# One lo part in six of the experts' weights, made by GpSimd instead of VectorE

## The chip, the core and the metric

The kernel runs on one core of a Trainium2 chip. The metric is device time in microseconds (us), the median of several executions. In the profile PE is TensorE's matmul, PEld its weight load, DVE is VectorE, ACT is ScalarE, POOL is GpSimd, SP is SyncE, which issues the loads.

## What is computed

Two layers of a decoder trunk for 272 tokens of width 1024: three token mixers side by side, then a channel mixer, dense in the first layer and a mixture of eight experts in the second. The change touches the experts alone. Each token goes to its two best experts; each expert is a gated network of 1024 x 3584, 1024 x 3584 and 3584 x 1024 weights in float32.

```python
def swiglu(h, w_gate, w_up, w_down):
    return (jax.nn.silu(h @ w_gate) * (h @ w_up)) @ w_down

    out = jnp.zeros_like(h)
    for e in range(N_EXPERTS):
        out = out + combine[..., e:e + 1] * swiglu(h, w_gate[e], w_up[e], w_down[e])
```

## The kernel before

Matmuls run on a reduced float type (fp32r). To keep float32's precision each weight is split in two: hi, the weight rounded to that type, and lo, the rest (weight minus hi). ACT makes hi (line 856), DVE makes lo from the raw weight and hi (line 857), and TensorE multiplies with both.

The experts come one after another, sorted by how many tokens they have: first a wide one (up to 128 tokens), then a narrow and a wide one in turn, and a narrow one (up to 64 tokens) last: four wide and four narrow. Each expert has 7 chunks of 512 hidden columns. A chunk needs 6 loads of 1 MB: two halves each of gate, up and down, issued by SP into 7 raw buffers (`wr`). A load is cut into two parts of 128x1024, each of which is one hi, one lo and the matmuls on them. So a chunk has 12 parts, which the text calls g0a g0b g1a g1b u0a u0b u1a u1b for gate and up, and d0a d0b d2a d2b for down; the down parts of a chunk follow the gate and up parts of the next. The names in the program are h_g_0, l_g_0 and so on: h for hi, l for lo, and both parts of one load have the same name. There are 8 x 7 x 12 = 672 parts. hi and lo have 7 buffers each (`HB`), in two pools of 5 and 2, so hi of a part waits until TensorE is through with the part seven before it.

In a wide expert TensorE makes six matmuls of 512 columns per part, in a narrow one four. When the gate parts of a chunk are through, ACT copies their sum out of PSUM; then the same is done for up. In a narrow expert these copies are gs (line 1124) and us (line 1125); TensorE turns both (hps, line 1133), ACT takes the sigmoid-weighted half s (line 78), DVE multiplies (s, line 1136), and ACT and DVE split the result into hi and lo for the down products (ht, lines 1139 and 1140). In a wide expert the steps are h (lines 78 and 1097), hps (1104), hth (1108) and htl (1109). When an expert is through, its result is added to the tokens' sums (yh, yl, hst, lines 1075 to 1081).

Each engine works through its own list in order. The framework's scheduler writes these lists from its own estimate of durations, so an edit in one line can change the order on several engines. A second pass over the experts (line 1195) runs only if an expert has more tokens than its width; in the profiled execution it doesn't run.

`nparts[0]` counts the parts. GpSimd has nothing to do in the experts' stage; its work (lines 177, 503, 647 to 672, 696, 736) lies in the stages before.

Of the kernel before, what the change touches and what calls it, by code (L numbers as in the profile page):

```python
# [9 lines left out]
F32 = mybir.dt.float32  # L10
# [5 lines left out]
ALU = mybir.AluOpType  # L16
# [35 lines left out]
def trunk(ctx: ExitStack, tc: tile.TileContext, x, meta, n1g, n2g, w_in, qng, kng, dlam,  # L52
# [3 lines left out]
    V, A, G, PE = nc.vector, nc.scalar, nc.gpsimd, nc.tensor  # L56
# [8 lines left out]
    def raw_ins(i):  # L65
        return getattr(i, "ins", i)
# [50 lines left out]
    with ExitStack() as lctx:  # L117
# [233 lines left out]
        for l in range(2):  # L351
# [226 lines left out]
            for hp in range(0, NH, 2):  # L578

                lgs = {}  # L580
                for X in (TA, TB):
# [5 lines left out]
                    for m in range(2):  # L587
                        b = m * 2 + hp // 2
                        pss = [ptile("lgps") for _ in range(2)]
                        for i in range(2):  # L590
                            r = 64 * i
# [86 lines left out]
            for bi, b in enumerate((1, 2, 0)):  # L678
                for half in range(2):
                    w = Weights(w_branch[l, b, :, half * 512:half * 512 + 512].rearrange("(k p) c -> p k c", p=P),  # L680
                                4, 512, f"br{l}{b}{half}")
                    for qd in range(2):
                        hi, lo = w.part(slice(0, 4), slice(qd * 256, qd * 256 + 256))
# [95 lines left out]
            for fp in range(NFD // 2):  # L779
# [3 lines left out]
                for j in range(2):  # L783
                    pss = []
                    for w in (wg, wu):
                        hi, lo = w.part(slice(0, KD), slice(j * P, (j + 1) * P))
# [18 lines left out]
            for cg in range(4):  # L805
                ps2 = [pp.tile([P, 512], F32, tag="pp", name=f"dn{j}") for j in range(2)]
                for f0 in range(0, NFD, 8):
# [3 lines left out]
                    for j in range(2):  # L811
                        hi, lo = w.part(slice(0, nf), slice(j * P, (j + 1) * P))
# [24 lines left out]
    nparts = [0]  # L837
    EARLY = 5

    class MoveWeights:  # L840
# [7 lines left out]
        def parts(self):  # L848
            st = 1024 // self.cols
            for k0 in range(0, self.nk, st):  # L850
                late = nparts[0] % HB >= HB - LATE
                wq, nb_ = (wqs[0], LATE) if late else (wqs[1], HB - LATE)
                hi = wq.tile([P, st, self.cols], F32R, tag="hi", bufs=nb_, name="h_" + self.name)
                lo = wq.tile([P, st, self.cols], F32R, tag="lo", bufs=nb_, name="l_" + self.name)
                r = self.raw[:, k0:k0 + st, :]
                ih = raw_ins(A.activation(hi, r, AF.Copy))  # L856
                il = raw_ins(V.tensor_tensor(lo, r, hi.bitcast(F32), op=ALU.subtract))  # L857
                nparts[0] += 1
                if EARLY < nparts[0] < 16:

                    tc.add_manual_dep(il, routed[0].name, nosync, reason="router")
                if EARLY < nparts[0] < 16:
                    tc.add_manual_dep(ih, last_in[0].name, nosync, reason="router")
                for k in range(st):
                    yield k0 + k, hi[:, k, :], lo[:, k, :]
# [360 lines left out]
```

## Time and profile before

| what | value |
|---|---|
| median of 3 runs | 1828.93 us (1828.43 to 1829.12) |
| the profiled execution | 1831.06 us, its span 1829.3 us |
| PE busy / DVE busy | 1763.9 us (96%) / 1468.0 us (80%) |
| ACT busy / POOL busy | 1179.2 us (64%) / 110.4 us (6%) |
| lo parts of the experts, line 857 | 3 groups (g, u, d) x 224, 1220 ns mean each |
| hi parts of the experts, line 856 | 3 groups x 224, 1052 to 1053 ns mean each |
| loads of the experts | 1024 KB each, 7.0 to 7.9 us from issue to landing |

How to read it: the shares are means over the whole span. The experts take the second half of it, some 990 us, and there the engines are much nearer to one another than the means show. A matmul's busy time overlaps with that of the next one, so PE's share says little. What sets the pace is read stage by stage, from the time of one chunk and from what ends the waits in it.

### The profile page before, as it was taken

The page shows a single profiled execution, that of the slowest core. Times are in us where ns is not written, and L with a number is a line of the kernel's source. Part 1 is how long each engine was busy: PE and PEld are TensorE (multiplying, and loading weights), DVE is VectorE, ACT ScalarE, POOL GpSimd, SP SyncE. Part 2 cuts the span into 40 slices and gives each one's busy share as a digit, 9 for nine tenths or more (in the row PEclk, how much of TensorE's full clock was granted, in tenths as well). Part 3 has the DMA queues.
Part 4 walks back from the last instruction along what each step waited for, and adds up shares of the span by engine and source line. Part 5 has one row for each costly group of instructions (what it writes and reads, how often), then busy time and mean ns, then how long its engine had stood idle before and what let it go on. Part 6 is the DMA issues. An engine that isn't in the chain of part 4 may idle for free.

```text
span 1829.3 us, 27972 instructions
## 1 busy us (share of the span) xinstructions
PE 1763.9 (96%) x10613; PEld 1515.4 (83%) x10613; DVE 1468.0 (80%) x1934; ACT 1179.2 (64%) x1587; POOL 110.4 (6%) x137
## 2 busy tenths in 40 slices
PE   8999999999999999999999999999999999999997
PEld 7888999999999889998788767776677866787665
DVE  7667757877567577577889999989998899988997
ACT  4366444544443664446778887768877688877786
POOL 5201201100011003012000000000000000000000
PEclk9999999999999999998999999999999999999999
DMA  7333554555554236656989999999999899999996
GB/s 214 101 99 93 169 177 162 165 181 185 167 179 139 70 95 189 187 196 234 343 321 368 366 394 371 360 330 352 394 387 372 315 345 395 394 351 352 362 388 232
DMA packets 266123, 479.96 MB, mean 262 GB/s; under 512 B 7636, under 2 KB 115228, under 8 KB 265980
## 3 DMA queue, kind: packets, MB, share of 16 engines
q1 hardware_dynamic: 265472, 477.20, 73.8%
q8 instruction: 85, 1.39, 0.3%
q0 software_dynamic: 368, 0.86, 0.2%
q14 instruction: 58, 0.48, 0.1%
q10 hardware_dynamic: 140, 0.04, 0.0%
HBM read 477.01 MB, written 1.05 MB: 261 GB/s over the span
## 4 chain that ended last, share of the span: by engine, by line
PE 49%; DVE 11%; issue 3%; ACT 3%; POOL 0%; DVEq 0%; ACTq 0%; POOLq 0%
DVE l_g L857 5%; PE psu L1119 4%; PE psu L1118 3%; PE y L1091 3%; PE y L1090 3%; PE y L1092 3%; PE psu L1091 3%; PE psg L1091 3%; PE psu L1092 3%; PE psu L1090 3%; PE psg L1092 2%; PE psg L1090 2%; PE proj L230 2%; PE proj L229 2%; PE proj L228 2%
## 5 line engine op out<-in xcount | busy, mean ns | idle before, releaser
L230 PE MATMUL proj<-hgh,lo_in 128*128 128x272 f32 (+1 forms) x1024 | 297.2, 290 | 4.6 <-DVE lo_in L224 4.6
L228 PE MATMUL proj<-hgh,hi_in 128*128 128x272 f32 (+1 forms) x1024 | 297.8, 291 | 0.2 <-DVE z L357 0.2
L229 PE MATMUL proj<-hgl,hi_in 128*128 128x272 f32 (+1 forms) x1024 | 296.9, 290 | 0.0
L857 DVE TENSOR_TENSOR l_u<-r_u,h_u 128x1024 fp32r<-128x1024 f32 x224 | 265.3, 1220 | 28.2 <-ACT h_u L856 25.1
L857 DVE TENSOR_TENSOR l_d<-r_d,h_d 128x1024 fp32r<-128x1024 f32 x224 | 264.8, 1220 | 17.4 <-ACT h_d L856 15.4
L857 DVE TENSOR_TENSOR l_g<-r_g,h_g 128x1024 fp32r<-128x1024 f32 x224 | 265.4, 1220 | 5.8 <-ACT h_g L856 5.4
L223 ACT ACTIVATE hi_in<-raw_in 128x1024 fp32r<-128x1024 f32 x128 | 135.0, 1058 | 165.6 <-PE proj L229 150.3
L856 ACT ACTIVATE h_u<-r_u 128x1024 fp32r<-128x1024 f32 x224 | 227.4, 1053 | 15.6 <-PE y L1092 9.0
L856 ACT ACTIVATE h_g<-r_g 128x1024 fp32r<-128x1024 f32 x224 | 226.5, 1053 | 11.9 <-PE psu L1092 5.4
L856 ACT ACTIVATE h_d<-r_d 128x1024 fp32r<-128x1024 f32 x224 | 223.2, 1052 | 7.1 <-PE psg L1092 5.9
L230 PEld LDWEIGHTS proj<-hgh,lo_in 128*128 128x128 f32 x1024 | 193.9, 189 | 6.6 <-DVE lo_in L224 5.5
L228 PEld LDWEIGHTS proj<-hgh,hi_in 128*128 128x128 f32 x1024 | 194.1, 190 | 2.8 <-issue 1.1
L229 PEld LDWEIGHTS proj<-hgl,hi_in 128*128 128x128 f32 x1024 | 193.6, 189 | 2.4 <-issue 1.3
L224 DVE TENSOR_TENSOR lo_in<-raw_in,hi_in 128x1024 fp32r<-128x1024 f32 x128 | 158.5, 1240 | 33.6 <-ACT hi_in L223 33.3
L1119 PE MATMUL psg<-l_g,x 128*128 128x512 f32 x224 | 98.7, 441 | 20.3 <-DVE l_g L857 20.0
L1119 PE MATMUL psu<-l_u,x 128*128 128x512 f32 x224 | 98.2, 438 | 1.5 <-DVE l_u L857 1.5
L1119 PEld LDWEIGHTS psg<-l_g,x 128*128 128x128 f32 x224 | 41.9, 187 | 63.3 <-DVE l_g L857 57.6
L1091 PE MATMUL psg<-l_g,x 128*128 128x512 f32 x224 | 91.2, 407 | 3.1 <-DVE l_g L857 2.8
L1090 PE MATMUL psg<-h_g,x 128*128 128x512 f32 x224 | 90.3, 403 | 0.0
L1118 PE MATMUL psu<-h_u,x 128*128 128x512 f32 x224 | 90.1, 402 | 0.0
L1090 PE MATMUL psu<-h_u,x 128*128 128x512 f32 x224 | 89.9, 401 | 0.0
L1092 PE MATMUL psg<-h_g,x 128*128 128x512 f32 x224 | 89.8, 401 | 0.0
(404 smaller groups left out, 4124.5 us busy)
## 6 DMA issues: line engine op xcount, KB each, us to landing
r_g<-in_moe_w_gate_dram SPq DMA_DIRECT2D x112, 1024.0 KB, 7.0
r_u<-in_moe_w_up_dram SPq DMA_DIRECT2D x112, 1024.0 KB, 7.7
r_d<-in_moe_w_down_dram SPq DMA_DIRECT2D x110, 1024.0 KB, 7.9
raw_in<-in_w_in_dram SPq DMA_DIRECT2D x64, 1024.0 KB, 5.9
raw_br<-in_w_branch_dram SPq DMA_DIRECT2D x12, 1024.0 KB, 5.5
raw_fg<-in_ffn_w_gate_dram SPq DMA_DIRECT2D x11, 1024.0 KB, 5.3
raw_fu<-in_ffn_w_up_dram SPq DMA_DIRECT2D x11, 1024.0 KB
raw_wo<-in_w_out_dram SPq DMA_DIRECT2D x8, 1024.0 KB, 4.9
```

The costliest lines, as they stand in the source:

```text
L223: A.activation(hi, r, AF.Copy)
L224: V.tensor_tensor(lo, r, hi.bitcast(F32), op=ALU.subtract)
L228: PE.matmul(ps, sh, mh, start=first, stop=False)
L229: PE.matmul(ps, sh, ml, start=False, stop=False)
L230: PE.matmul(ps, sl, mh, start=False, stop=last)
L856: ih = raw_ins(A.activation(hi, r, AF.Copy))
L857: il = raw_ins(V.tensor_tensor(lo, r, hi.bitcast(F32), op=ALU.subtract))
L1090: PE.matmul(ps, st[0], hi, start=first, stop=False)
L1091: PE.matmul(ps, st[0], lo, start=False, stop=False)
L1092: PE.matmul(ps, st[1], hi, start=False, stop=last)
L1118: PE.matmul(ps, st[0], hi, start=first, stop=False)
L1119: PE.matmul(ps, st[0], lo, start=False, stop=last)
```

## The change

From the third chunk on (part 24), every part whose number leaves 3 when divided by 6 has its lo made by GpSimd (`G`) instead of VectorE (`V`). In a chunk these are g0b and u1b. In the pass that runs these are 108 of the 672 lo parts: two in each of 54 chunks.

```diff
@@ -854,7 +854,8 @@
                 r = self.raw[:, k0:k0 + st, :]
                 ih = raw_ins(A.activation(hi, r, AF.Copy))
-                il = raw_ins(V.tensor_tensor(lo, r, hi.bitcast(F32), op=ALU.subtract))
+                eng = G if nparts[0] >= 24 and nparts[0] % 6 == 3 else V
+                il = raw_ins(eng.tensor_tensor(lo, r, hi.bitcast(F32), op=ALU.subtract))
                 nparts[0] += 1
```

Lines behind it are one higher in the changed kernel (857 is 858, 1125 is 1126). SP's list is the same in both. The other lists change as follows.

VectorE in a middle chunk of the first narrow expert, before, from u0b on:

```order
L857 TENSOR_TENSOR l_u_0_11399<-r_u_0_11388,h_u_0_11398 128x1024
L857 TENSOR_TENSOR l_u_1_11409<-r_u_1_11406,h_u_1_11408 128x1024
L857 TENSOR_TENSOR l_u_1_11417<-r_u_1_11406,h_u_1_11416 128x1024
L857 TENSOR_TENSOR l_d_0_11431<-r_d_0_11428,h_d_0_11430 128x1024
L857 TENSOR_TENSOR l_d_0_11439<-r_d_0_11428,h_d_0_11438 128x1024
L857 TENSOR_TENSOR l_d_2_11449<-r_d_2_11446,h_d_2_11448 128x1024
L857 TENSOR_TENSOR l_d_2_11457<-r_d_2_11446,h_d_2_11456 128x1024
L1136 TENSOR_TENSOR s<-s,hps 128x256
```

VectorE at the same place now, up to the next chunk's first part:

```order
L858 TENSOR_TENSOR l_u_0_11399<-r_u_0_11388,h_u_0_11398 128x1024
L858 TENSOR_TENSOR l_u_1_11409<-r_u_1_11406,h_u_1_11408 128x1024
L858 TENSOR_TENSOR l_d_0_11431<-r_d_0_11428,h_d_0_11430 128x1024
L858 TENSOR_TENSOR l_d_0_11439<-r_d_0_11428,h_d_0_11438 128x1024
L1137 TENSOR_TENSOR s<-s,hps 128x256
L858 TENSOR_TENSOR l_d_2_11449<-r_d_2_11446,h_d_2_11448 128x1024
L858 TENSOR_TENSOR l_d_2_11457<-r_d_2_11446,h_d_2_11456 128x1024
L1141 TENSOR_TENSOR ht<-s,ht 128x4x64
L858 TENSOR_TENSOR l_g_0_11468<-r_g_0_11465,h_g_0_11467 128x1024
```

The second lo of u1 is gone from VectorE's list, and s has moved from behind d2b to behind d0b. ht, which stood behind the next chunk's g0b, now stands ahead of its g0a.

ScalarE in the same chunk, before:

```order
L856 ACTIVATE h_u_1_11416<-r_u_1_11406 128x1024
L856 ACTIVATE h_d_0_11430<-r_d_0_11428 128x1024
L856 ACTIVATE h_d_0_11438<-r_d_0_11428 128x1024
L1125 ACTIVATE us<-psu 128x512
L856 ACTIVATE h_d_2_11448<-r_d_2_11446 128x1024
L856 ACTIVATE h_d_2_11456<-r_d_2_11446 128x1024
L78 ACTIVATE s<-hps 128x256
```

ScalarE now:

```order
L856 ACTIVATE h_u_1_11416<-r_u_1_11406 128x1024
L856 ACTIVATE h_d_0_11430<-r_d_0_11428 128x1024
L1126 ACTIVATE us<-psu 128x512
L856 ACTIVATE h_d_0_11438<-r_d_0_11428 128x1024
L78 ACTIVATE s<-hps 128x256
L856 ACTIVATE h_d_2_11448<-r_d_2_11446 128x1024
L856 ACTIVATE h_d_2_11456<-r_d_2_11446 128x1024
L1140 ACTIVATE ht<-s 128x4x64
```

us has moved ahead of hi of d0b, and s ahead of hi of d2a and d2b. On TensorE the turns of us (hps, line 1133, four in a row now, two and two before) have moved ahead of lo of d0a.

GpSimd's list before has nothing in the experts' pass; now it holds lo of u1b and of g0b in turn, 108 of them.

## Rows read from the trace of the kernel before

**Rows 1.** Windows: stretch, length; PE, PEld, DVE, ACT, POOL busy; PE clock; DMA
```profile
840.00:850.00 10.00, 7.31 (x56) 6.48 (x55) 6.55 (x21) 5.04 (x11) 3.58 (x9) 0.82 0.53 201
850.00:860.00 10.00, 10.00 (x40) 9.29 (x41) 8.27 (x39) 3.92 (x11) 0.00 (x0) 0.50 0.33 107
941.34:958.22 16.88, 16.88 (x77) 13.92 (x76) 15.63 (x15) 13.70 (x14) 0.00 (x0) 1.00 1.00 371
1270.65:1285.93 15.28, 14.51 (x65) 10.23 (x65) 14.47 (x16) 13.36 (x17) 0.00 (x0) 1.00 1.02 381
1330.48:1459.05 128.57, 124.89 (x566) 99.92 (x566) 111.88 (x115) 94.14 (x111) 0.00 (x0) 1.00 0.97 358
1459.05:1572.31 113.26, 106.76 (x476) 76.69 (x475) 106.27 (x107) 95.02 (x117) 0.00 (x0) 1.00 1.00 372
```

**Rows 2.** Chain of work that ended last, a narrow expert: start, length, what
```profile
1270.65 2.27 DVE l_g L857 x2
...
1285.93 2.27 DVE l_g L857 x2
```

**Rows 3.** Timeline of DVE, one narrow chunk: start, length, what [idle before <-releaser]
```profile
1504.79 2.36 DVE L857 TENSOR_TENSOR l_u<-r_u,h_u 128x1024 fp32r<-128x1024 f32 x2 [0.46 <-ACT h_u L856]
...
1509.79 2.36 DVE L857 TENSOR_TENSOR l_d<-r_d,h_d 128x1024 fp32r<-128x1024 f32 x2 [0.37 <-ACT h_d L856]
1512.07 0.42 DVE L1136 TENSOR_TENSOR s<-s,hps 128x256 f32<-128x256 f32 x1
...
1515.01 2.35 DVE L857 TENSOR_TENSOR l_g<-r_g,h_g 128x1024 fp32r<-128x1024 f32 x2
...
1520.09 1.23 DVE L857 TENSOR_TENSOR l_u<-r_u,h_u 128x1024 fp32r<-128x1024 f32 x1 [0.46 <-ACT h_u L856]
```

**Rows 4.** Timeline of ACT, the same narrow chunk
```profile
1508.21 0.60 ACT L1125 ACTIVATE us<-psu 128x512 f32<-128x512 f32 x1 [0.60 <-PE psu L1119]
1508.71 1.99 ACT L856 ACTIVATE h_d<-r_d 128x1024 fp32r<-128x1024 f32 x2
1510.91 0.39 ACT L78 ACTIVATE s<-hps 128x256 f32<-128x256 f32 x1 [0.21 <-PE hps L1133]
...
1518.42 0.69 ACT L1124 ACTIVATE gs<-psg,ws 128x512 f32<-128x512 f32 x1 [1.14 <-PE psg L1119]
1519.01 2.00 ACT L856 ACTIVATE h_u<-r_u 128x1024 fp32r<-128x1024 f32 x2
```

**Rows 5.** Timeline of PE, the same narrow chunk: the turns of us
```profile
1509.40 0.56 PE L1133 MATMUL hps<-ii,us 128*128 128x64 f32 x4
...
1510.32 0.55 PE L1133 MATMUL hps<-ii,us 128*128 128x64 f32 x4
```

**Rows 6.** Timeline of DVE, a wide chunk: g0a and g0b
```profile
942.57 2.46 DVE L857 TENSOR_TENSOR l_g<-r_g,h_g 128x1024 fp32r<-128x1024 f32 x2
```

**Rows 7.** Timeline of PE, the same wide chunk: first product with lo of g0b
```profile
950.93 0.39 PE L1091 MATMUL psg<-l_g,x 128*128 128x512 f32 x1
```

**Rows 8.** Timeline of POOL, in the stages before the experts
```profile
289.91 1.63 POOL L696 TENSOR_TENSOR mx<-mx,gt 128x272 f32<-128x272 f32 x2 [82.85 <-DVE gt L695]
...
688.82 2.55 POOL L647 TENSOR_TENSOR cc<-cc,ch 128x1088 f32<-128x1088 f32 x1 [83.79 <-DVE ch L357]
...
702.77 3.25 POOL L658 TENSOR_TENSOR y<-y,cbt 128x1024 f32<-128x1024 f32 x1 [4.64 <-DVE cbt L357]
...
831.47 1.77 POOL L736 TENSOR_TENSOR ssq<-ssq,sq 128x256 f32<-128x256 f32 x1 [2.87 <-ACT sq L735]
```

**Rows 9.** Timeline of DVE, at the same times
```profile
290.25 0.44 DVE L695 TENSOR_TENSOR gt<-br,gt 128x272 f32<-128x272 f32 x1 [0.48 <-PE br L230]
...
689.27 3.19 DVE L224 TENSOR_TENSOR lo_in<-raw_in,hi_in 128x1024 fp32r<-128x1024 f32 x1 [0.53 <-ACT hi_in L223]
...
702.54 1.21 DVE L224 TENSOR_TENSOR lo_in<-raw_in,hi_in 128x1024 fp32r<-128x1024 f32 x1
...
832.57 1.75 DVE L857 TENSOR_TENSOR l_g<-r_g,h_g 128x1024 fp32r<-128x1024 f32 x1
```

## The prediction

> **What bounds the kernel now.** I read the windows first, by stage, because the page's shares mix stages with different limits. A wide expert takes 128.57 us and a narrow one 113.26 [rows 1], each 7 chunks; what differs is who waits. In a middle chunk of a wide expert (16.88 us) PE is busy for all of it and DVE for 15.63. In a middle chunk of a narrow one (15.28 us) DVE is busy for 14.47 and PE has holes [rows 1]. The chain of waits agrees: in the narrow experts it comes back every 15.28 us to DVE making lo of the gate parts [rows 2].
>
> Next the timelines of one narrow chunk. DVE runs through but for two waits, 0.46 and 0.37 us, both for ACT's hi [rows 3]. ACT is late there because it is itself held: it waits 0.60 us for the last up product before us, and 1.14 us for the last gate product before gs [rows 4], and both products wait for DVE's lo. So the narrow chunk is a loop: lo of the last gate part, products, gs, hi of u1a, lo of u1a, and on through us and s to the next gate parts. Whatever makes a lo in this loop later makes the chunk longer; only 0.83 us of DVE's time in it is idle. The wide chunk has a reserve instead: DVE ends lo of g0b at 942.57 + 2.46 = 945.03 [rows 6], PE first uses it at 950.93 [rows 7], 5.9 us later.
>
> **What a lo costs on GpSimd.** No GpSimd work stands in the experts' stage; the nearest rows are its two-input operations of the same size in the stages before. One of 128x1024 has a record of 3.25 us from 702.77, but DVE's lo_in ran from 702.54 to 703.75, and the rest, 706.02 - 703.75, is 2.27 us. One of 128x1088 that started with DVE idle took 2.55 [rows 8, 9], or 2.40 scaled to 1024. I take 2.27. On DVE a lo takes 1.23, and 1.14 from start to start in a row (pairs of 2.36 and 2.35 [rows 3]).
>
> The same rows show that the two engines don't work side by side. DVE's lo_in that began at 689.27, during the 2.55 us of GpSimd, took 3.19: it ended at 692.46, 1.09 us after GpSimd's end at 691.37. At 831.47 GpSimd came while DVE was in a lo, and the next lo on DVE (from 832.57) took 1.75, ending 1.08 after GpSimd's 833.24. So a DVE operation on two SBUF tiles waits for GpSimd's whole operation, GpSimd waits for the one that DVE is in, and a waiting GpSimd comes before DVE's next. DVE's gt at 290.25, with one input in PSUM, took its 0.44 us beside GpSimd [rows 8, 9].
>
> The Trainium skill (SBUF — State Buffer, Who interferes with whom) states this as a rule: a VectorE instruction with two SBUF inputs contends with a GpSimd instruction that reads SBUF, and the one that issued first holds the shared ports to its end. The trace agrees (3.19 us instead of some 1.2). By the rule alone, without the loop that follows, the sum would be the 37 us of the second rival.
>
> So a lo that is moved takes 1.14 us from DVE's list and puts 2.27 + 1.08 - 1.14 = 2.21 us in its way: each costs DVE 1.07, where the edit reads as a relief.
>
> **The narrow chunk, step by step.** Time 0 is the start of lo of u1a on DVE (before: 1504.79). Lo of u1a ends at 1.23. GpSimd has hi of u1b by then (ACT is one part ahead), takes the ports and ends at 3.50; before, this lo ended at 2.36. From there to us before it was 1508.21 - 1507.15 = 1.06 us (products, then ACT) [rows 3, 4]: us starts at 4.56, ends at 5.16. Its turns on PE follow. Before, s on ACT began 2.10 after us ended [rows 4], with down products between; the turns alone are two halves of 0.55 and their loads [rows 5], so now between 1.2 and 2.1; I take 1.6, as they are now in one piece. s starts at 6.76. Hi of d2a stands behind it on ACT, starts 0.28 later, takes 1.05, and lo of d2a starts 0.04 after that (as 1509.79 follows hi from 1508.71 [rows 3, 4]), at 8.13. Lo of d2a and d2b: 2 x 1.14 = 2.28. ht on DVE, as small as s with its record of 0.42 [rows 3], of which the next operation overlaps some 0.08 as in the pairs: 0.34, to 10.75. Lo of the next g0a: 1.22, to 11.97. GpSimd's g0b: 2.27, to 14.24. Lo of g1a, held until then: 1.08; g1b: 1.14, to 16.46. Then 1.06 to gs (1518.42 - 1517.36 [rows 3, 4]), 0.59 from gs to hi of u1a, 1.05 + 0.04 for that hi: the next lo of u1a starts at 19.20. Before, it was 1520.09 - 1504.79 = 15.30 [rows 3]. So +3.9 us per middle chunk. Of it about 2.2 is GpSimd's hold, and the rest comes from the new order: us and s now stand ahead of the hi parts of d0b and d2 on ACT, and wait there for products that GpSimd made late, while DVE has nothing to do (lo of d0b can't start before 6.15).
>
> There are 4 x 5 = 20 such chunks: 78 us. The first chunk of each narrow expert has the same order: 4 x 3.9 = 15.6. In the second the old expert's sums stand behind g0a on DVE (yl, hst, with a PSUM input each), which can run beside GpSimd, and s keeps its old place; I take 1.5 each: 6. In all 100.
>
> **The wide experts.** 14 lo parts of each move (10 in the first expert's last five chunks), which is 14 x 1.07 = 15 us more for DVE. It has 128.57 - 111.88 = 16.7 us idle per expert [rows 1], and behind g0b in the middle chunks stands h, with a PSUM input, which runs beside GpSimd. The 5.9 us of reserve cover one late lo of 1 to 2 us. The first chunks after a narrow expert have no reserve yet. So between 0 and 12 us each; I take 3.5, nearer to nothing since the middle chunk has cover: 4 x 3.5 = 14, rounded down to 13 for the first expert.
>
> SP's list is the same. The raw buffers come free later, but nothing in the rows of DVE and ACT above waits for a load, and a slower narrow chunk asks for less per us. Code for the second pass doesn't run.
>
> **Sum.** 100 + 13 = 113 us. The profiled execution was 1831.06 (span 1829.3 and 1.8 around it), which becomes 1944; it lies 2.1 above the median of the three runs, so 1942 there.
>
> **Rivals.**
> 1. GpSimd doesn't hold DVE, only its own duration counts. Then GpSimd starts u1b when its hi is there, at 0.99, and ends at 3.26, 0.24 earlier than above; what follows is as above up to g0a, but g0b is off the path: lo of g1a starts when its hi is there (12.0, four hi parts of 0.95 behind s and ht), and lo of g1b ends at 14.36 instead of 16.46. That is 2.1 less: 17.1 a chunk, +1.8. 24 x 1.8 + 4 x 0.5 = 45: 1874. Against it stand the four overlaps in [rows 8, 9].
> 2. The hold is real, but other work fills the gaps of the new order. Then only DVE's sum counts: 2 x 1.07 - 0.83 idle = 1.31 a narrow chunk, x 28 = 37: 1866.
> 3. The clock falls. PE gets more holes in the narrow chunks. Once before, after a stretch with 7.31 us busy of 10, the granted clock was 0.50 for a while [rows 1], which is 1.2 GHz. If that came in each narrow chunk, the links on PE alone (1.06 twice, 1.6) would double: +3.7 x 28 = 104, so 2046. In the narrow chunks before, with holes too, it was 1.00.
> 4. The relief works: DVE, the busiest engine of the narrow chunk, loses two of twelve lo parts, and the chunk falls to ACT's busy time, 13.36 [rows 1]: -1.9 x 28 = -53, so 1776. The deciding point is GpSimd's duration: without any hold the chunk is 17.1 at 2.27 us, and us follows it one for one, so it gains only below 2.27 - 1.8 = about 0.5 us. No row of this size is near that. The Trainium skill (Perfetto Trace Analysis, Optimizing Scalar/DVE Operations) allows moving work to GPSIMD where DVE is saturated, and says in the same place that it might not help, because of the shared port. Here the trace speaks for the second half.
>
> **Chances.** Forecast (1905 to 1978) 0.67; rivals 1 and 2 with what lies around them (1860 to 1905) 0.17; rival 3 or longer loops (above 1978) 0.11; no change 0.02; faster 0.03. The range goes from rival 2 at 1866 to 1978, which is the forecast with turns of 2.1 instead of 1.6 (+12) and 12 us instead of 3.5 in two or three wide experts. A measurement here can tell about 0.2%, some 4 us: faster 0.03, same 0.02, slower 0.95.
>
> **What would show it.** In the changed profile: GpSimd's lo with records of 2.3 us and more; DVE's lo in two kinds, 1.2 us and, behind GpSimd, up to 3.2; narrow middle chunks of 19 us, with DVE waiting for hi of d0b and d2a, and ACT for some 2 us before us; wide middle chunks still at about 16.9. Narrow chunks near 17 with DVE at 1.2 throughout would mean rival 1, near 16.7 rival 2; a granted clock of 0.5 in them, rival 3. What I am least sure of is the 1.6 for the turns and the wide experts' start.

## The result and the profile after

| | before | after |
|---|---|---|
| median, 4 runs each side by side | 1829.03 us | 1948.46 us (1947.13 to 1951.59) |
| profiled execution, span | 1831.06, 1829.3 us | 1951.59, 1949.5 us |

The change makes the kernel slower: the ratio is 1.0646, 95% interval 1.0633 to 1.0659. The forecast was 1942.

The page of the changed kernel, its line of busy time and the groups of the experts' lo parts (columns: line, engine, operation, count, busy time and mean of one in ns, idle time ahead and its releaser):

```profile
PE 1798.7 (92%) x10613; PEld 1516.9 (78%) x10613; DVE 1501.8 (77%) x1826; ACT 1180.3 (61%) x1587; POOL 397.3 (20%) x245
...
L858 DVE TENSOR_TENSOR l_d<-r_d,h_d 128x1024 fp32r<-128x1024 f32 x223 | 331.1, 1515 | 87.7 <-ACT h_d L856 86.8
...
L858 DVE TENSOR_TENSOR l_g<-r_g,h_g 128x1024 fp32r<-128x1024 f32 x171 | 262.3, 1561 | 14.0 <-ACT h_g L856 13.9
...
L858 POOL TENSOR_TENSOR l_g<-r_g,h_g 128x1024 fp32r<-128x1024 f32 x53 | 150.1, 2831 | 382.2 <-ACT h_g L856 216.1
L858 POOL TENSOR_TENSOR l_u<-r_u,h_u 128x1024 fp32r<-128x1024 f32 x54 | 134.0, 2482 | 407.9 <-ACT h_u L856 395.1
```

DVE issues 108 operations fewer than before, and yet is busy for 1501.8 us instead of 1468.0: its d and g parts, 1220 ns each before, are now recorded with means of 1515 and 1561. That time is not work. The groups also show which parts moved: 53 of g, 54 of u and one of d (223 of its 224 are left on DVE). So it is two in a chunk with two exceptions: in the third chunk of all only u1b moves, and in the very last chunk a down part moves as well.

Windows of the changed kernel: a wide middle chunk of the first expert, a narrow middle chunk, a wide and a narrow expert (stretch and length; PE, PEld, DVE, ACT, POOL busy; clock; DMA share and GB/s). They answer to [rows 1].

```profile
941.97:958.87 16.90, 16.90 (x77) 13.91 (x76) 14.61 (x13) 13.69 (x15) 4.83 (x2) 1.00 1.01 371
...
1613.79:1632.50 18.71, 15.38 (x66) 10.12 (x66) 15.76 (x13) 13.37 (x17) 5.24 (x2) 1.00 0.94 346
...
1386.87:1525.45 138.58, 128.71 (x568) 100.95 (x569) 115.83 (x104) 94.50 (x110) 36.41 (x14) 0.99 0.90 319
1525.45:1659.94 134.49, 112.72 (x474) 76.86 (x472) 112.93 (x90) 95.03 (x116) 36.51 (x14) 0.99 0.93 327
```

The wide middle chunk is where it was (16.88), the narrow one has gone from 15.28 to 18.71, a narrow expert from 113.26 to 134.49, a wide one from 128.57 to 138.58. Added up over all, from each expert's first hi to the next expert's, the narrow ones take 91 us more and the wide ones 29; the sum is the 120 by which the two spans differ.

That narrow chunk on GpSimd, on VectorE and on ScalarE (start, length, what, idle before and its releaser), which answers to [rows 3, 4]:

```profile
1614.83 2.41 POOL L858 TENSOR_TENSOR l_u<-r_u,h_u 128x1024 fp32r<-128x1024 f32 x1 [6.00 <-ACT h_u L856]
1624.69 2.83 POOL L858 TENSOR_TENSOR l_g<-r_g,h_g 128x1024 fp32r<-128x1024 f32 x1 [7.45 <-PE y L1120]
```

```profile
1613.79 1.23 DVE L858 TENSOR_TENSOR l_u<-r_u,h_u 128x1024 fp32r<-128x1024 f32 x1 [0.47 <-ACT h_u L856]
1615.68 2.64 DVE L858 TENSOR_TENSOR l_d<-r_d,h_d 128x1024 fp32r<-128x1024 f32 x1 [0.67 <-ACT h_d L856]
1619.87 1.23 DVE L858 TENSOR_TENSOR l_d<-r_d,h_d 128x1024 fp32r<-128x1024 f32 x1 [1.54 <-ACT h_d L856]
1621.01 0.42 DVE L1137 TENSOR_TENSOR s<-s,hps 128x256 f32<-128x256 f32 x1
1621.45 2.36 DVE L858 TENSOR_TENSOR l_d<-r_d,h_d 128x1024 fp32r<-128x1024 f32 x2
...
1624.06 1.22 DVE L858 TENSOR_TENSOR l_g<-r_g,h_g 128x1024 fp32r<-128x1024 f32 x1
1625.54 4.21 DVE L858 TENSOR_TENSOR l_g<-r_g,h_g 128x1024 fp32r<-128x1024 f32 x2 [0.26 <-ACT h_g L856]
...
1632.47 1.23 DVE L858 TENSOR_TENSOR l_u<-r_u,h_u 128x1024 fp32r<-128x1024 f32 x1 [0.46 <-ACT h_u L856]
```

```profile
1618.29 0.60 ACT L1126 ACTIVATE us<-psu 128x512 f32<-128x512 f32 x1 [2.64 <-PE psu L1120]
1618.78 1.05 ACT L856 ACTIVATE h_d<-r_d 128x1024 fp32r<-128x1024 f32 x1
1620.08 0.39 ACT L78 ACTIVATE s<-hps 128x256 f32<-128x256 f32 x1 [0.25 <-PE hps L1134]
...
1630.80 0.69 ACT L1125 ACTIVATE gs<-psg,ws 128x512 f32<-128x512 f32 x1 [2.45 <-PE psg L1120]
```

Read it along the clock. DVE ends lo of u1a at 1615.02; GpSimd ends u1b at 1617.24, 2.22 us later. DVE's lo of d0a is recorded from 1615.68 but ends at 1618.32, 1.08 after GpSimd: it did nothing until GpSimd was through. ACT waits 2.64 us for psu, in part since u1b was late (with the new order but without GpSimd it is 1.55, see below); hi of d0b stands behind us, and so DVE idles for 1.54 us. At 1624.69 the same begins again with g0b.

### The profile page after: what moved, and what is told of

The parts are those of the page before. It is cut to its first block, busy times and chain, and to the rows that moved or that the text cites. A ratio compares the mean times of both kernels' runs of the same rounds, so it can differ in the third digit from the quotient of the medians.

```text
span 1949.5 us, 28137 instructions
## 1 busy us (share of the span) xinstructions
PE 1798.7 (92%) x10613; PEld 1516.9 (78%) x10613; DVE 1501.8 (77%) x1826; ACT 1180.3 (61%) x1587; POOL 397.3 (20%) x245
## 3 DMA queue, kind: packets, MB, share of 16 engines
HBM read 477.01 MB, written 1.05 MB: 245 GB/s over the span
## 4 chain that ended last, share of the span: by engine, by line
PE 40%; POOL 9%; DVE 8%; ACT 7%; issue 4%; POOLq 0%; ACTq 0%; DVEq 0%
POOL l_g L858 4%; POOL l_u L858 4%; ACT h_u L856 4%; DVE l_d L858 3%; PE psg L1120 3%; PE psg L1092 2%; PE psg L1093 2%; PE psg L1091 2%; PE proj L229 2%; PE proj L230 2%; PE proj L228 2%; PE psu L1092 2%; PE y L1120 2%; PE y L1092 2%; PE psu L1093 2%
## 5 line engine op out<-in xcount | busy, mean ns | idle before, releaser
L858 DVE TENSOR_TENSOR l_d<-r_d,h_d 128x1024 fp32r<-128x1024 f32 x223 | 331.1, 1515 | 87.7 <-ACT h_d L856 86.8
L858 DVE TENSOR_TENSOR l_u<-r_u,h_u 128x1024 fp32r<-128x1024 f32 x170 | 218.2, 1314 | 32.7 <-ACT h_u L856 32.5
L858 POOL TENSOR_TENSOR l_g<-r_g,h_g 128x1024 fp32r<-128x1024 f32 x53 | 150.1, 2831 | 382.2 <-ACT h_g L856 216.1
L858 POOL TENSOR_TENSOR l_u<-r_u,h_u 128x1024 fp32r<-128x1024 f32 x54 | 134.0, 2482 | 407.9 <-ACT h_u L856 395.1
L1120 PE MATMUL psu<-l_u,x 128*128 128x512 f32 x224 | 99.9, 446 | 30.1 <-POOL l_u L858 24.0
L1092 PE MATMUL psu<-l_u,x 128*128 128x512 f32 x224 | 91.6, 409 | 9.5 <-POOL l_u L858 5.6
L1092 PE MATMUL y<-l_d,hth 128*128 128x512 f32 x224 | 89.8, 401 | 4.3 <-DVE l_d L858 4.3
```

Of the source, the lines that this page charges most:

```text
L858: il = raw_ins(eng.tensor_tensor(lo, r, hi.bitcast(F32), op=ALU.subtract))
L1092: PE.matmul(ps, st[0], lo, start=False, stop=False)
L1120: PE.matmul(ps, st[0], lo, start=False, stop=last)
```

## The experiments

All medians are beside runs of the kernel before on the same chip (1829.2 to 1829.3); brackets hold the 95% interval of the ratio.

### Is it the hold on the ports?

**A second copy.** All lists of DVE, ACT and TensorE are those of the kernel before; GpSimd makes the 108 lo parts once more, into a scratch tile (in bf16) that nobody reads.

```diff
                 il = raw_ins(V.tensor_tensor(lo, r, hi.bitcast(F32), op=ALU.subtract))
+                if nparts[0] >= 24 and nparts[0] % 6 == 3:
+                    again = mo.tile([P, st, self.cols], BF16, tag="again", bufs=1, name="again")
+                    G.tensor_tensor(again, r, hi.bitcast(F32), op=ALU.subtract)
```

> VectorE makes every lo, as before, and all lists of ScalarE, VectorE and TensorE are those of before; GpSimd makes the 108 chosen lo parts once more, into a scratch tile that nothing reads. Theory 1 (GpSimd's two-input operation holds VectorE's two-input operations off for its whole duration): each copy puts 2.2 us into VectorE's list; a narrow middle chunk goes from 15.3 to 18.5-19 us (14.5 busy + 4.4), lo records on VectorE of about 3.4 us stand behind GpSimd's, a wide expert loses what its 16.7 us of idle DVE time doesn't cover of 14 x 2.2 = 31: about 1980 us, 1930 at least. Theory 2 (the new order and GpSimd's duration on the path make the loss, nothing is held): 1829 within 5, lo records 1.22 us throughout.

Measured: 2062.19 us, ratio 1.1262 [1.1243, 1.1281]. No product waits for GpSimd's copy (only the buffers of raw and hi do, to come free), and still the time rises by 233 us: GpSimd's reading holds DVE back. In DVE's timeline a pair of lo that GpSimd falls into takes 4.55 us, not 2.36 (GpSimd's row, then DVE's):

```profile
1341.46 2.42 POOL L860 TENSOR_TENSOR again<-r_u,h_u 128x1024 bf16<-128x1024 f32 x1 [8.66 <-ACT h_u L856]
```

```profile
1340.41 4.55 DVE L857 TENSOR_TENSOR l_u<-r_u,h_u 128x1024 fp32r<-128x1024 f32 x2 [1.66 <-ACT h_u L856]
```

It is also 80 us more than expected. Windows of two narrow chunks, and the line of the run's span and mean clock:

```profile
1392.05:1411.69 19.64, 14.61 (x65) 10.21 (x65) 18.81 (x15) 13.34 (x18) 4.95 (x2) 1.00 0.88 320
1328.26:1350.55 22.29, 16.94 (x63) 12.31 (x62) 19.48 (x15) 13.33 (x18) 4.84 (x2) 0.85 0.83 302
```

```profile
core 0: 2061.4 us, clock 0.951
```

At a full clock the chunk is 19.64 us, what 15.3 and two holds of 2.19 (4.55 - 2.36) give (19.7); of the sixteen regular narrow chunks of this run it is the only one that kept that clock. Where TensorE's granted clock fell to 1.2 GHz for part of the chunk (mean 0.85) it is 22.29. Over the run the mean clock is 0.951 where it was 0.993: of full-speed time 0.049 x 2061 = 101 us are missing, 13 before. That is about the 80 us, by this estimate; the loss of clock was seen beside it, not switched off.

**Fills instead of a subtract.** The same lists; GpSimd reads one column of hi (so that it starts at the same time) and then fills the scratch tile twice, which only writes.

```diff
+                    G.tensor_copy(again[:, 0, 0:1], hi[:, 0, 0:1].bitcast(F32))
+                    for _ in range(2):
+                        G.memset(again, 0.0)
```

> As the kernel before in all lists but GpSimd's; GpSimd reads one column of hi of the 108 chosen parts (so that it starts at the same point) and then fills a scratch tile of 128x1024 twice, without reading. Theory 1 (only operations that read SBUF hold VectorE's second input): 1829 to 1845 us, VectorE's lo records about 1.22 us beside the fills. Theory 3 (anything GpSimd does holds VectorE): fills of 0.95 us each, 2 x 0.95 in VectorE's list per part: 1930 us or more.

Measured: 1833.13 us, 1.0019 [1.0009, 1.0029]. Its groups of fills and of DVE's lo:

```profile
L862 POOL MEMSET again<- 128x1024 bf16 x216 | 205.6, 952 | 12.6
...
L857 DVE TENSOR_TENSOR l_u<-r_u,h_u 128x1024 fp32r<-128x1024 f32 x224 | 265.3, 1219 | 28.2 <-ACT h_u L856 25.1
```

GpSimd is as busy over the run as in the change (414.8 us, 397.3 there), and DVE's lo stays at 1219 ns; 196 of the lo parts overlap a fill in the trace, and none of these took longer than 1.23 us. So GpSimd's being at work costs next to nothing (4 us, at the limit of what can be measured); its reading does. This is what the Trainium skill (SBUF — State Buffer, Who interferes with whom) states: a VectorE instruction with two SBUF inputs contends with a GpSimd instruction that reads, not with one that only writes.

### How much is the hold, how much the new order?

**The old order with GpSimd.** The change, with us put back behind hi of d0b and s behind hi of d2b.

```diff
+            def late():
+                i = raw_ins(A.activation(us, psu, AF.Copy))
+                tc.add_manual_dep(i, last_hi[0].name, nosync, reason="order")
...
-            act(s, hps[:, 0:256], AF.Silu)
+            i = act(s, hps[:, 0:256], AF.Silu)
+            if last_d[0] is not None:
+                tc.add_manual_dep(i, last_d[0].name, nosync, reason="order")
```

> The change, with ScalarE's and VectorE's lists of the narrow chunk put back to those of before (us behind hi of d0b, s behind hi of d2b; ht behind g0a on VectorE), by order alone. Theory 1 with the loop of the prediction: us no longer holds up hi of d0b, s no longer hi of d2a; by the same walk the chunk is 17.4 us instead of 18.7, 24 such chunks: 1917 us (1905 to 1930). If the hold alone made the loss and the order nothing: 1946 to 1950. If the order made all of it: under 1850.

**The new order without GpSimd.** The kernel before, with us forced between hi of d0a and hi of d0b; the scheduler then puts s where the change has it.

```diff
+                    if late and j == 0:
+                        late()
...
+                if last_us[0] is not None:
+                    tc.add_manual_dep(ih, last_us[0].name, nosync, reason="order")
```

> The kernel before, DVE makes all lo parts and GpSimd none; in a narrow expert ACT and DVE walk in the order that the scheduler chose for the change (us behind the hi of d0a instead of d0b, s between d0b and d2a). Theory 1 (the order costs by itself: the hi of d0b stands behind us, and us behind psu, so DVE idles some 1.6 us before d0b in place of 0.37 before d2a): narrow middle chunk 16.4 to 16.75 instead of 15.29, 25 to 37 us: 1858 us (1850 to 1868). Rival (the order costs only because GpSimd's u1b makes psu late): narrow chunk 15.3, 1826 to 1834 us.

Measured: the old order with GpSimd 1928.22 us, 1.0532 [1.0515, 1.055]; the new order alone 1856.74, 1.0142 [1.0127, 1.0158]. A narrow middle chunk in each (windows; the old order with GpSimd first):

```profile
1579.69:1597.14 17.45, 14.64 (x66) 10.29 (x66) 15.90 (x12) 13.34 (x17) 4.96 (x2) 1.00 0.99 362
```

```profile
1534.23:1550.78 16.55, 15.32 (x66) 10.11 (x66) 14.56 (x15) 13.35 (x17) 0.00 (x0) 1.00 1.04 393
```

Before, the regular narrow chunks take 15.29 us in the mean, in the change 18.69. The hold costs 17.45 - 15.29 = 2.16 us a chunk, which is twice 2.22 - 1.14 = 1.08, and the order 16.55 - 15.29 = 1.26. Together 3.42; the change measures 18.69 - 15.29 = 3.40. So in these chunks the two add, and neither needs the other. Over the whole run they come to 99 + 28 = 127 us, for 119 of the change; where they overlap was not followed. Without GpSimd the order's price is to be seen as a wait of DVE for hi of d0b, where the kernel before has 0.37 us (before d2a); ACT waits for psu there, too: it is idle for 1.55 us before the copy us (DVE's row, then ACT's):

```profile
1539.23 1.23 DVE L863 TENSOR_TENSOR l_d<-r_d,h_d 128x1024 fp32r<-128x1024 f32 x1 [1.49 <-ACT h_d L858]
```

```profile
1537.65 0.60 ACT L1135 ACTIVATE us<-psu 128x512 f32<-128x512 f32 x1 [1.55 <-PE psu L1127]
```

**One part at a time.** GpSimd makes only g0b (first line), or only u1b (second).

```diff
+                eng = G if nparts[0] >= 24 and nparts[0] % 12 == 9 else V
```

```diff
+                eng = G if nparts[0] >= 24 and nparts[0] % 12 == 3 else V
```

> The change with GpSimd making only g0b (53 parts); u1b stays with DVE. In this kernel the rows of DVE and ACT in a narrow chunk stand as in the kernel before (s behind d2b, us behind d0b), so only the hold is left. Theory 1 (each lo on GpSimd costs DVE's walk GpSimd's 2.22 us less the 1.14 us that DVE no longer works, and the order is a second cost of its own that comes with u1b): narrow middle chunk 15.29 + 1.08 = 16.37 us, some 28 x 1.1 = 31 us in the narrow experts and half of wide_only's 26 us in the wide ones: 1873 us (1865 to 1880). Rival (the two parts cost alike, order and all): half of the change's 119 us, 1889 us (1883 to 1895), narrow chunk 17.0.

> The change with GpSimd making only u1b (54 parts); g0b stays with DVE. The scheduler's order is that of the change (s between d0b and d2a, us behind d0a). Theory 1: one hold and the whole of the order's cost, narrow middle chunk 15.29 + 1.08 + 1.24 = 17.6 us, 28 x 2.3 = 65 us, and 13 us in the wide experts: 1907 us (1898 to 1915). Rival (the two parts cost alike): 1889 us (1883 to 1895), narrow chunk 17.0.

Measured: 1879.99 us, 1.0271 [1.0255, 1.0287], and 1904.07, 1.0402 [1.0386, 1.0418]. Narrow chunks of g0b alone, then of u1b alone:

```profile
1286.04:1303.24 17.20, 15.60 (x65) 11.52 (x65) 15.52 (x14) 13.35 (x18) 2.55 (x1) 0.90 1.00 352
...
1824.86:1841.20 16.34, 14.58 (x65) 10.25 (x65) 15.52 (x14) 13.35 (x18) 2.54 (x1) 1.00 1.04 392
```

```profile
1575.00:1592.62 17.62, 15.38 (x65) 10.08 (x64) 14.92 (x14) 13.34 (x17) 2.40 (x1) 1.00 0.99 356
```

At a full clock g0b alone gives 16.34, one hold (expected 16.37); u1b alone 17.62, one hold and the order (expected 17.6). g0b alone ends 7 us above the expected 1873: eight of its narrow chunks, in three experts, ran like the first line, with a mean clock of 0.90 and 0.86 us longer.

**Half a part.** Of each of these parts DVE makes the first 512 columns, GpSimd the rest.

```diff
+                if st == 2 and nparts[0] >= 24 and nparts[0] % 6 == 3:
+                    for half, eng in enumerate((V, G)):
+                        eng.tensor_tensor(lo[:, half, :], r[:, half, :], hi[:, half, :].bitcast(F32), op=ALU.subtract)
...
```

> The change with each of GpSimd's 107 parts split in two: DVE makes the first 512 of the 1024 columns, GpSimd the second; the order on ACT is that of the change. Theory 1 (DVE stands still for as long as GpSimd's own subtract lasts): GpSimd's piece 1.1 to 1.3 us instead of 2.22, DVE's piece some 0.6, so each part costs DVE's walk some 0.6 instead of 1.08: narrow middle chunk 15.3 + 2 x 0.6 + the order's 1.2 = 17.7 us, 67 us in the narrow experts and half of 26 in the wide ones: 1909 us (1895 to 1920). Rival (what costs is the handing over, whatever GpSimd does with it): DVE works 0.6 more than in the change and waits the same, narrow chunk 19.3 or more, 1955 us or more.

Measured: 1905.77 us, 1.0419 [1.0403, 1.0435]. The pieces of one u1b:

```profile
1601.92 1.33 POOL L859 TENSOR_TENSOR l_u<-r_u,h_u 128x512 fp32r<-128x512 f32 x1 [6.59 <-ACT h_u L856]
```

```profile
1602.02 1.78 DVE L859 TENSOR_TENSOR l_u<-r_u,h_u 128x512 fp32r<-128x512 f32 x1
```

GpSimd ends at 1603.25, DVE's piece 0.55 later, and the next chunk begins 17.66 us after this one. The hold is as long as GpSimd's own work: half the columns, half the excess (0.55 a part). It is no fixed toll for handing over.

### Which experts pay?

The change in the wide experts alone (51 parts), and in the narrow ones alone (57; the same line with `Narrow`):

```diff
+                eng = G if nparts[0] >= 24 and nparts[0] % 6 == 3 and kind_now[0] is Wide else V
```

> GpSimd makes the chosen lo parts of the wide experts alone (52), VectorE those of the narrow ones. In the changed kernel the last three wide experts are 8 to 10 us longer each, 29 in all. If their own 14 lo parts cost that: 1858 us (1850 to 1865), the narrow experts' middle chunks at 15.3. If it is carried over from the slower narrow experts ahead of them, whose end leaves TensorE no reserve: 1829 to 1836.

> The change with GpSimd at work in the narrow experts alone (57 parts). If each kind of expert pays for its own parts: the change's 1948 less the 26 us that GpSimd in the wide experts alone cost, 1922 us (1915 to 1928), narrow middle chunk 18.69 as in the change. If the wide experts' later lengths in the change came with what the narrow ones had left behind: under 1910.

Measured: 1855.13 us, 1.0144 [1.0127, 1.0161], and 1916.04, 1.0474 [1.0458, 1.049]. The two excesses, 26 and 87, make 113 of the change's 119; each kind pays for its own parts. What the wide ones pay stands in TensorE's timeline, the waits for a lo over 0.25 us in the second wide expert's first chunks, with GpSimd in the wide experts alone and then in the kernel before:

```profile
1099.09 0.50 PE L1093 MATMUL psu<-l_u,x 128*128 128x512 f32 x1 [0.59 <-POOL l_u L859]
...
1109.45 0.50 PE L1093 MATMUL psg<-l_g,x 128*128 128x512 f32 x1 [0.88 <-POOL l_g L859]
...
1117.39 0.51 PE L1093 MATMUL psu<-l_u,x 128*128 128x512 f32 x1 [1.88 <-DVE l_u L859]
...
1127.93 0.50 PE L1093 MATMUL y<-l_d,hth 128*128 128x512 f32 x1 [0.43 <-DVE l_d L859]
```

```profile
1112.79 0.50 PE L1091 MATMUL psg<-l_g,x 128*128 128x512 f32 x1 [0.32 <-DVE l_g L857]
```

Before, TensorE waited 0.32 us for a lo in this stretch; now 3.8, at GpSimd's parts and at lo parts of DVE that come behind them. In the change itself the same four waits are 0.60, 0.89, 1.88 and 0.46 us. TensorE was busy for 97% of a wide expert before, so it has little idle time to take them up: over the expert shown in the windows its idle time goes from 128.57 - 124.89 = 3.7 us to 138.58 - 128.71 = 9.9. The rest of that expert's 10 us stands in its matmuls' records and was not followed.

### What does bound the narrow chunk, and is there a gain?

The prediction calls the narrow chunk a loop with 0.83 us of idle DVE in it. Three kernels without GpSimd try to take these 0.83 us: gs and us are put behind later hi parts on ACT; gs alone; and both with s behind hi of g0b as well (the lines are of the third).

```diff
+            ig = raw_ins(A.activation(gs, psg, AF.Copy, scale=self.g.ws[:, 1, 1:2]))
+            tc.add_manual_dep(ig, self.u1a.name, nosync, reason="order")
...
+                    if late and j == 2:
+                        late()
...
+            if g0b[0] is not None:
+                tc.add_manual_dep(i, g0b[0].name, nosync, reason="order")
```

> The kernel before, without GpSimd; in a narrow expert gs is put behind the hi of u1b on ACT and us behind the hi of d2a, so that DVE's two waits in a narrow chunk (0.46 us before u1a, 0.37 us before d2a, both for a hi that stood behind gs or us) should go. Theory 1 (DVE's walk with its waits sets a narrow chunk): middle chunk 14.47 instead of 15.29, 20 to 28 chunks x 0.8 = 16 to 22 us, 1807 to 1813 us. Rival (the transfers, at a share of 1.02 to 1.04 in a narrow chunk, or PE at 14.51 of 15.28 us, set it just as tightly): 1822 to 1830 us.

> The kernel before, without GpSimd; only gs is moved, behind the hi of u1b on ACT (us stays behind the hi of d0b). Theory 1 (DVE's walk sets the narrow chunk, and the 0.46 us wait before u1a goes without a new one, since us and the turns keep their places): middle chunk 14.83, 24 to 28 chunks x 0.46 = 11 to 13 us: 1817 us (1813 to 1821). Rival (the turns' matmuls of TensorE come later, as with both moved, or the transfers bind): 1826 to 1836 us.

> The kernel before, without GpSimd; in a narrow expert gs is behind the hi of u1b and us behind the hi of d2a (as with both moved), and s behind the hi of g0b, so that no hi waits for TensorE's turns any more. Theory 1 (DVE's work, 14.47 us, and TensorE's, 14.46 us, are the only floors; the 0.83 us are the loop from the turns over s and the hi of g0a back to TensorE): middle chunk 14.5 to 14.8, 26 x 0.65 = 17 us: 1812 us (1806 to 1819). Rival (the transfers, at a share of 1.04 in these chunks, allow no shorter one): 15.2 to 15.3, 1824 to 1831 us.

Measured: 1836.93 us, 1.0048 [1.0035, 1.0062]; 1829.94, 1.0002 [0.9993, 1.0011]; and 1810.77, 0.9911 [0.9895, 0.9927]. The first two expectations failed (with both moved even the rival's 1822 to 1830). DVE's waits with both moved, then with gs alone:

```profile
1509.74 0.42 DVE L1148 TENSOR_TENSOR s<-s,hps 128x256 f32<-128x256 f32 x1 [0.77 <-ACT s L78]
1510.68 2.36 DVE L859 TENSOR_TENSOR l_g<-r_g,h_g 128x1024 fp32r<-128x1024 f32 x2 [0.52 <-ACT h_g L857]
```

```profile
1508.73 2.36 DVE L859 TENSOR_TENSOR l_d<-r_d,h_d 128x1024 fp32r<-128x1024 f32 x2 [0.60 <-ACT h_d L857]
...
1511.65 2.36 DVE L859 TENSOR_TENSOR l_g<-r_g,h_g 128x1024 fp32r<-128x1024 f32 x2 [0.23 <-ACT h_g L857]
```

With gs alone the waits before u1a and d2a, 0.46 + 0.37, have become 0.60 + 0.23 at other places: the same 0.83, and the same 15.30 us. With both moved they are 1.29. What held was the way from us over TensorE's turns and s to hi of g0a, which stands behind s on ACT. The third kernel takes hi of g0a and g0b out of that way (on TensorE the turns of us come in one piece with it; the two were not tried apart):

```profile
1499.62:1513.91 14.29, 14.03 (x66) 10.41 (x65) 14.29 (x15) 13.34 (x17) 0.00 (x0) 1.00 1.04 392
```

```profile
1502.56 4.62 DVE L860 TENSOR_TENSOR l_u<-r_u,h_u 128x1024 fp32r<-128x1024 f32 x4
1507.10 4.62 DVE L860 TENSOR_TENSOR l_d<-r_d,h_d 128x1024 fp32r<-128x1024 f32 x4
```

DVE now runs without a gap, 14.29 us a chunk. This version beats both kernels, by 0.9% the one before. The rival of these runs, the transfers, falls for the middle chunks: at a share of 1.04 (1.02 in the chunk of [rows 1]) they carried the shorter chunk.

## Why the prediction was right, and where it was off

**The hold: right.** GpSimd's lo ends 2.22 and 2.24 us after DVE's (the prediction took 2.27 from lo_in), DVE's next ends 1.08 to 1.09 after that (1.08), and each moved part costs 1.08 (1.07). The second copy, the fills and the halves show it from three sides. Of the four overlaps that the prediction sets against its first rival, three show the hold; the fourth, gt with its input in PSUM, shows the exception.

**The narrow chunk: right in mechanism, 19.20 against 18.69.** The links of the sum: u1b to us 1.05 (1.06), s to lo of d2a 1.37 (1.37), g1b to gs 1.05 (1.06), DVE held until 1.09 after GpSimd (1.08). The step that failed is the turns: s starts at 1620.08, 1.19 after us ends at 1618.89, where 1.6 was taken between ends of 1.2 and 2.1. It was the lower end: in one piece and ahead of lo of d0a the turns wait for nothing on TensorE. That and the 0.05 and 0.03 by which GpSimd was quicker are the whole 0.5. The split, 2.2 for the hold and the rest (1.7) for the order, measures 2.16 and 1.26. The reason given for the rest is right in part only: us and s, it says, wait for products that GpSimd made late. The new order without GpSimd costs the same 1.26, so us stands too early for its products in any case.

Twenty middle chunks cost 68 us instead of 78, the first chunks 11.5 instead of 15.6, the second ones 9.4 instead of 6: 89 in all, for 100 (the other 2 of the 91 lie behind the last chunk). The first and second chunks were not as forecast, either. Of the 11.5 us 6.9 come from one chunk, in which GpSimd did not come next (last section); the other three took 0.9 to 2.1 more, where 3.9 was taken, and why stays open. Two of the second chunks cost 3.3 each at a mean granted clock of 0.92, the two at 1.00 cost 1.2 and 1.6, about the 1.5 of the prediction.

**The wide experts: under-sized, 13 against 29.** The middle chunks of the first expert are untouched, as said. The step that failed is to take their reserve of 5.9 us for typical. In the three later wide experts TensorE waits at the parts that were late (shown above with GpSimd in the wide experts alone), and these take 8.4, 10.0 and 10.2 us more, near the 12 of the upper bound; the 3.5 chosen fitted none. The errors of 11 and 16 us nearly cancel by luck, and the forecast is closer than its parts.

**The rivals.** No hold (1874) is refuted by the second copy. Only DVE's sum (1866) is refuted by the new order alone, which costs 28 us without GpSimd: the gaps were not filled. The relief (1776) didn't come. The clock (2046) is a matter of degree. In the change it stayed at 1.00 in the regular narrow chunks and fell in some of the first and second ones (mean of the run 0.987, 0.993 before: 0.013 x 1950 - 0.007 x 1829 = some 12 us of full speed, an estimate). In the second copy and with g0b alone it did fall, and cost what the windows there show.

**What the sum says of DVE's idle time.** The prediction counts 0.83 us of idle as the only cover in the narrow chunk, and g0b alone shows that even that covers nothing: 16.34 is 15.29 and all but 0.03 of the hold. The idle belongs to a loop through TensorE and ACT; the last three kernels show which.

## What to carry to other kernels

By what is measured here, on float32 subtracts of 128x1024 and 128x512, an operation with two SBUF inputs that is moved from VectorE to GpSimd relieves VectorE only if nothing with two SBUF inputs has to run there meanwhile: price it as GpSimd's duration less VectorE's, per part, on VectorE's path. After such an edit compare the order of every engine before the durations: here over a third of a narrow chunk's loss came from a copy that the scheduler put one place earlier, and from what followed it. And where an engine idles a little in every round, look for the loop that makes it wait before counting the idle time as cover or as gain.

## What the runs showed that was not expected

**GpSimd doesn't always come next.** The prediction holds that a waiting GpSimd comes before DVE's next operation. Of some 86 parts in the change at which GpSimd came during such an operation of DVE, it did not once, in the first chunk of the second narrow expert, and at the same place with the old order put back (7.74 us there too). The same is to be seen twice with u1b alone (records of 7.75 us, from 1128.60 and 1393.06) and twice with the halves (7.27 and 6.90 us):

```profile
1248.13 7.74 POOL L858 TENSOR_TENSOR l_g<-r_g,h_g 128x1024 fp32r<-128x1024 f32 x1 [6.93 <-ACT h_g L856]
```

```profile
1247.91 3.49 DVE L858 TENSOR_TENSOR l_g<-r_g,h_g 128x1024 fp32r<-128x1024 f32 x3
1251.32 2.35 DVE L858 TENSOR_TENSOR l_u<-r_u,h_u 128x1024 fp32r<-128x1024 f32 x2
```

DVE made five lo parts without a gap, each at full speed, and GpSimd began only when they were through: 5.5 us late, and TensorE waited 5.54 us for its part. That chunk took 25.09 us instead of 18.23, at a mean granted clock of 0.86. Why DVE went on here and gave way elsewhere stays open.

**The clock can fall chunk by chunk.** With g0b alone the mean granted clock was 0.90 in one 17.20 us chunk, with TensorE busy for 15.60 us of it, and 1.00 in a 16.34 us chunk of the same instructions with 14.58 us busy. So the same list ran in two ways within one execution; what tipped it was not isolated.
